# Moving the products of head rows with their inverse norms from VectorE to GpSimd in a two-layer decoder trunk

## The chip, the cores and the metric

The kernel runs on one core of a Trainium2 chip. The metric is the time of one execution on the device in microseconds (us). The core has a matrix engine (TensorE, PE in the profile; PEld is its weight load), VectorE (DVE), ScalarE (ACT), GpSimd (POOL), SyncE (SP), and DMA queues. SP issues most loads; POOL issues one kind of DMA, described below.

## The reference

Two layers are run over a sequence of 256 tokens with width 2048. Each layer has two groups of eight heads that share one input projection and one output projection, and an MLP of 8192:

```
h    = rms_norm(x, attn_norm)
proj = h @ w_in            # g_q g_k g_v g_gate g_lr | s_q s_k s_v
log_a = log_sigmoid(g_lr @ w_gate_up + b_gate) / 16
o_gla = gla_chunked(heads(g_q), heads(g_k), heads(g_v), heads(log_a))
o_gla = rms_norm(o_gla, gla_out_norm) * silu(g_gate)        # norm per head
sq, sk = rms_norm(heads(s_q), sb_q_norm), rms_norm(heads(s_k), sb_k_norm)
o_sb  = rms_norm(stick_breaking_attention(sq, sk, heads(s_v)), sb_out_norm)
x = x + concat(o_gla, o_sb) @ w_o
x = x + square(relu(rms_norm(x, mlp_norm) @ w_up)) @ w_down
```

A head has 128 columns. Four tensors in each layer are therefore normalised head by head: the stick-breaking queries, their keys, their outputs, and the outputs of the gated linear attention (GLA).

## The kernel before

Everything is float32. A large product is made of three matmuls of parts: each operand is split into a high part and the low rest, and high times high, high times low and low times high are summed (L1243 to L1245 for the narrow products of the input projection, with the weight parts `whi` and `wlo`). SP loads raw weights; ACT makes `whi` (L868); DVE makes `wlo` as raw minus `whi` (L872). In the MLP some low parts, `dlo`, are made another way: ACT writes the negated high part (L876) and a DMA that POOL issues adds the raw weights to it (L879).

All work of a layer is written as pieces of a `Plan`: a piece has an engine, an assumed length, the pieces that it depends on and the buffers that it takes and frees. `Plan.run` gives each piece a due time. PE's pieces that are written in line are due one after the other at their assumed lengths; a piece on another engine is due in time for its earliest user. Then `run` plays the pieces through: DVE and ACT take the ready piece with the earliest due time; PE, SP and POOL take the pieces of their `line` in the order in which they were written. PE pieces that are set `apart` (turns, scores, and so on of the attention) go ahead of PE's line as soon as they are ready in the plan. The order that comes out is fixed on every engine; at run time semaphores alone hold an engine back. Inside the attention stage, `core` adds pieces of the attention, `into_bank` adds a PE piece that writes into a PSUM bank, `aside` one that is set apart.

`heads_norm(rows, w)` norms rows of 128 tokens by `w` columns, that is `w`/128 heads: ACT squares each row (L1348), DVE sums each head's squares (L1351), `inv_rms` makes the inverse root of the mean (DVE L459, ACT, then three short DVE steps at L466 to L468 that refine it), and `mul_heads` multiplies the row by its heads' inverse norms (L1330, one DVE tensor_tensor of 128x512 a row). The kernel runs it on pairs of rows of 512 columns for keys and queries (512 columns is four heads, so twice for eight heads), on the stick-breaking outputs `on`, and on the GLA outputs: 16 products in each layer. Whoever uses a row waits for its product: `heads_turn` transposes keys and queries on PE (L1378) for the scores; the outputs `on` and the GLA outputs, those after a multiplication with the gate (DVE), are transposed into the output projection's operand (`to_operand`, PE L1519).

The gates of the GLA need the low-rank columns `lr`: DVE scales them (L2021), PE turns them (L1681), DVE copies the result into `lrT` (L1687), and PE multiplies it by `wg` (L1701). POOL makes masks and cleared tiles at the start of a layer and memsets of the padded GLA operands `act` and `t` (L1792, L1793, L1891), and copies decay factors `dec` (L1747).

Of the kernel before, what the change touches and what calls it, by code (L numbers as in the profile page):

```python
# [33 lines left out]
FASTR = (1, 3, 4, 5, 6)  # L34
ADDEDR = (2, 7)
FIRSTR = 1
STEPSI = [0, 0, 1, 3, 1, 2, 2, 1, 1, 3, 4, 4, 5, 5, 5, 6, 5, 6, 6, 6, 7, 7]
FASTI = (1, 5, 6)
ADDEDI = ADDED
# [22 lines left out]
class Plan:  # L62
# [48 lines left out]
    def release(self, hold, *pieces):  # L111
        for p in Plan.flat(pieces):
            p.frees.append(hold)
            hold.left += 1

    def run(self, stock):
        for p in self.pieces:
            p.deps = Plan.flat([p.deps, p.after])
            for d in p.deps:
                d.users.append(p)  # L120
        t = 0.0
        for p in self.pieces:
            if p.engine == "PE":
                t += p.length
                p.due = t - p.length
        wait = {p: len(p.deps) for p in self.pieces}
        topo = [p for p in self.pieces if not p.deps]
        for p in topo:
            for u in p.users:
                wait[u] -= 1  # L130
                if not wait[u]:
                    topo.append(u)
        assert len(topo) == len(self.pieces)
        for p in reversed(topo):
            if p.engine != "PE" or p.apart:
                p.due = min([u.due for u in p.users], default=t) - p.length - p.lag - self.GAP
        for p in self.pieces:
            if p.core:
                p.due -= EARLY
        line = {  # L140
            e: [p for p in self.pieces if p.engine == e and not p.apart]
            for e in ("PE", "SP", "POOL")
        }
        free = dict.fromkeys(("PE", "SP", "POOL", "DVE", "ACT", "NONE"), 0.0)
        left = {p: len(p.deps) for p in self.pieces}
        at = dict.fromkeys(self.pieces, 0.0)
        ready = {"DVE": [], "ACT": [], "NONE": [], "APART": []}
        pool = {k: list(v) for k, v in stock.items()}
        order, events, count = [], [], 0
        for p in self.pieces:  # L150
            if not p.deps:
                events.append((0.0, count, p))
                count += 1
        came = set()

        def fits(p):
            return all(
                sum(h.kind == k for h in p.takes) <= len(v) for k, v in pool.items()
            ) if p.takes else True

        def first_fit(heap):
            put_back, got = [], None
            while heap:
                c = heapq.heappop(heap)
                if fits(c[2]):
                    got = c[2]
                    break
                put_back.append(c)
            for c in put_back:
                heapq.heappush(heap, c)  # L170
            return got

        while events:
            now, _, p = heapq.heappop(events)
            if isinstance(p, Plan.Piece):
                e = "APART" if p.apart else p.engine
                if e in ready:
                    heapq.heappush(ready[e], (p.due, count, p))
                else:
                    came.add(p)  # L180
                count += 1
            elif p is not None:
                for h in p:
                    pool[h.kind].append(h.m)
            for e in free:
                if free[e] > now + 1e-9:
                    continue
                p = first_fit(ready[e]) if e in ready else None
                if e == "PE":
                    p = first_fit(ready["APART"])  # L190
                if not p and e in line and line[e] and line[e][0] in came and fits(line[e][0]):
                    p = line[e].pop(0)
                if not p:
                    continue
                for h in p.takes:
                    h.m = pool[h.kind].pop(0)
                order.append(p)
                free[e] = now + p.length
                heapq.heappush(events, (free[e], count, None))
                count += 1  # L200
                got = p.gives
                for h in p.frees:
                    h.left -= 1
                    if not h.left:
                        got = got + [h]
                if got:
                    heapq.heappush(events, (free[e] + p.lag + self.GAP, count, got))
                    count += 1
                for u in p.users:
                    gap = self.SAME.get(e, 0.0) if u.engine == e else self.GAP  # L210
                    if u.apart and u.engine != e:
                        gap += self.CALM
                    at[u] = max(at[u], free[e] + p.lag + gap)
                    left[u] -= 1
                    if not left[u]:
                        heapq.heappush(events, (at[u], count, u))
                        count += 1
        assert len(order) == len(self.pieces)
        for p in order:
            if p.fn:  # L220
                p.fn()
        return max(free.values())
# [3 lines left out]
def trunk_kernel(  # L226
# [17 lines left out]
    nc = tc.nc  # L244
# [57 lines left out]
    def t2_tile(hold=None, shape=(P, 512)):  # L302
        if hold is None:
            m = turn_of[0] = (turn_of[0] + 1) % T2
        else:
            m = hold.m
        return tpool.tile(list(shape), F32, tag=f"t2_{m}", name=nm("t"), bufs=1)
# [426 lines left out]
    def lazy(make):  # L734

        box = []

        def get():
            if not box:
                box.append(make())  # L740
            return box[0]

        return get
# [39 lines left out]
    def unit_order(u):  # L783

        if u.kind == "o":
            return (STEPSO, STEPSP)[u.n2], (FASTO0, FASTO)[u.n2]
        if u.kind in ROWS[FIRSTR:]:
            return STEPSR, FASTR
        if u.kind == ROWS[0]:
            return STEPSI, FASTI  # L790
        return STEPS, FAST
# [477 lines left out]
    def core(engine, length, fn, *deps, lag=0.0):  # L1269
        p = add(engine, length, fn, *deps, opened["att"], lag=lag)  # L1270
        p.core = True
        using["att"].append(p)
        return p
# [38 lines left out]
    def norm_tile(key, hold, n):  # L1312
        tile_ = spool.tile([P, 8], F32, tag=f"{key}{hold.m}", name=nm("st"), bufs=1)
        return tile_[:, :n]
# [11 lines left out]
        b = core("ACT", 0.42, lambda: box["parts"][1](), a)  # L1326
        return (lambda: box["rr"]), core("DVE", 0.72, lambda: box["parts"][2](), b)

    def mul_heads(dst, src, rr, nh):
        nc.vector.tensor_tensor(  # L1330
            dst.rearrange("p (h d) -> p h d", d=P),
            src.rearrange("p (h d) -> p h d", d=P),
            rr.unsqueeze(2).to_broadcast([P, nh, P]),
            ALU.mult,
        )

    def heads_norm(rows, w, *deps):

        nh = w // P
        slot_hold = Plan.Hold("norm")  # L1340
        ss = lazy(lambda: norm_tile("ns", slot_hold, len(rows) * nh))
        got = []
        for i, (row, dep) in enumerate(rows):
            hold = Plan.Hold("t2")
            sq = lazy(lambda hold=hold: t2_tile(hold))

            def square(row=row, sq=sq):
                nc.scalar.activation(sq()[:, :w], row(), AF.Square)  # L1348

            def total(i=i, sq=sq):  # L1350
                nc.vector.tensor_reduce(  # L1351
                    ss()[:, i * nh : (i + 1) * nh],
                    sq()[:, :w].rearrange("p (h d) -> p h d", d=P), AX.X, ALU.add,
                )

            a = core("ACT", 0.2 + w * 8.3e-4, square, dep, *deps)
            a.takes.append(hold)
            got.append(core("DVE", 0.14 + w * 1.06e-3, total, a, got))
            release(hold, got[-1])
        got[0].takes.append(slot_hold)  # L1360
        rr, ready = inv_rms(ss, len(rows) * nh, P, slot_hold, got)
        muls = [
            core(
                "DVE", 0.15 + w * 1.06e-3,
                lambda i=i, row=row: mul_heads(row(), row(), rr()[:, i * nh : (i + 1) * nh], nh),
                ready,
            )
            for i, (row, _) in enumerate(rows)
        ]
        release(slot_hold, muls)  # L1370
        return muls
# [796 lines left out]
```

## Time and profile before

| | |
|---|---|
| median of three runs | 2127.96 us (2127.22 to 2128.28) |
| the profiled execution | 2126.1 us |
| its span | 2124.3 us |
| PE busy | 2113.5 us, 99% |
| DVE busy | 1970.3 us, 93% |
| ACT busy | 1599.6 us, 75% |
| POOL busy | 175.6 us, 8% |
| granted TensorE clock | 1.0 |

The span is the time between the first and the last instruction of the profile; what the execution takes beyond it is the launch around it. A share is the busy time over the span. The two attention stages, where all products of inverse norms lie, are at about 198 to 305 us and 1234 to 1330 us. A row of a group has line, engine, operation, output<-inputs with partitions x elements, the count, then busy us and mean ns of one. A row of a timeline has start, length, engine and line; what stands in brackets at its end is the idle time before it and what ended that.

### The profile page before, as it was taken

What the parts mean: (1) busy time and instruction counts of PE and PEld (TensorE: products, weight loads), DVE (VectorE), ACT (ScalarE), POOL (GpSimd) and SP (SyncE); (2) the same over time, 40 slices, a digit from 0 to 9 for tenths busy, and PEclk for the clock granted to TensorE, in tenths of its full rate; (3) what the DMA queues carried; (4) which work ended last, traced back from release to release, by engine and by line L of the source; (5) the groups of instructions that cost most, each with busy time, mean ns of one, the idle gap of its engine ahead of it and who ended that gap; (6) DMA issues with size and microseconds to landing.
All of it is one profiled execution on the core that took longest, in us unless ns stands there. A gap on an engine that the chain in (4) does not pass through costs nothing.

```text
span 2124.3 us, 28632 instructions
## 1 busy us (share of the span) xinstructions
PE 2113.5 (99%) x10043; PEld 1759.2 (83%) x10043; DVE 1970.3 (93%) x2672; ACT 1599.6 (75%) x2082; POOL 175.6 (8%) x234
## 2 busy tenths in 40 slices
PE   9999999999999999999999999999999999999999
PEld 8888888888888888888888888888888888888887
DVE  7998889999999999999999987899999999999998
ACT  7776878787678677678787776878876776786775
POOL 0111000000000000000010101000000000000000
PEclk9999999999999999999999999999999999999999
DMA  8897347888888888878888762778888888888786
GB/s 302 246 269 197 128 150 229 253 255 254 268 235 257 241 251 253 268 240 248 234 249 261 222 204 80 224 232 250 262 241 256 254 241 272 236 256 249 250 246 177
DMA packets 160723, 501.35 MB, mean 236 GB/s; under 512 B 14298, under 2 KB 23074, under 8 KB 160580
## 3 DMA queue, kind: packets, MB, share of 16 engines
q1 hardware_dynamic: 135236, 407.25, 55.2%
q0 software_dynamic: 25344, 92.29, 23.0%
q8 instruction: 79, 1.29, 0.2%
q14 instruction: 64, 0.52, 0.1%
HBM read 405.12 MB, written 2.10 MB: 192 GB/s over the span
## 4 chain that ended last, share of the span: by engine, by line
PE 96%; DMA 2%; ACT 1%; DVE 1%; issue 0%; POOLq 0%; DVEq 0%
DMA dlo<-raw 2%; ACT whi L868 0%; PE m__462_2282 L1243 0%; PE m__468_2294 L1243 0%; PE m__2547_12117 L1243 0%; PE m__2549_12123 L1243 0%; DVE wlo L872 0%; DVE act L749 0%; PE m__12_144 L668 0%; PE m__12_144 L667 0%; PE m__579_2863 L1243 0%; PE m__13_145 L667 0%; PE m__579_2863 L1244 0%; PE m__462_2282 L1245 0%; PE m__2473_11750 L1245 0%
## 5 line engine op out<-in xcount | busy, mean ns | idle before, releaser
L868 ACT ACTIVATE whi<-raw 128x1024 fp32r<-128x1024 f32 (+2 forms) x944 | 900.6, 969 | 331.7 <-issue 57.7
L872 DVE TENSOR_TENSOR wlo<-raw,whi 128x1024 fp32r<-128x1024 f32 (+1 forms) x768 | 830.5, 1086 | 69.8 <-ACT whi L868 61.1
L879 POOL DMA_DIRECT2D dlo<-raw x176 | 150.2, 855 | 1760.7 <-ACT dlo L876 974.9
L868 ACT ACTIVATE whi<-ts 128x1024 fp32r<-128x1024 f32 x176 | 186.4, 1059 | 82.4 <-DVE ts L749 5.9
L872 DVE TENSOR_TENSOR wlo<-ts,whi 128x1024 fp32r<-128x1024 f32 x176 | 214.6, 1219 | 6.4 <-ACT whi L868 5.0
L749 DVE TENSOR_TENSOR ts<-raw 128x1024 f32<-128x1024 f32 x176 | 214.6, 1220 | 1.9
L876 ACT ACTIVATE dlo<-raw 128x1024 fp32r<-128x1024 f32 x176 | 180.8, 1046 | 7.8 <-PE m__2004_9526 L968 1.7
L749 DVE TENSOR_TENSOR raw<-raw 128x512 f32<-128x512 f32 x176 | 120.7, 686 | 1.7
L749 DVE TENSOR_TENSOR raw<-ts,raw 128x512 f32<-128x512 f32 x176 | 120.3, 683 | 0.2
L1106 ACT ACTIVATE act<-act,st 128x512 f32<-128x512 f32 x96 | 66.4, 713 | 30.9 <-DVE act L749 30.6
L541 DVE TENSOR_TENSOR act<-t,act 128x512 fp32r<-128x512 f32 (+1 forms) x97 | 60.9, 635 | 0.1
L537 ACT ACTIVATE act<-t 128x512 fp32r<-128x512 f32 (+1 forms) x97 | 55.7, 583 | 0.4
L1351 DVE TENSOR_REDUCE st<-t 128x4 f32<-128x512 f32 x32 | 21.1, 680 | 7.1 <-ACT t L1348 7.1
L749 DVE TENSOR_TENSOR xb<-t,xb 128x512 f32<-128x512 f32 x40 | 27.3, 683 | 0.2
L610 ACT ACTIVATE t<-xb 128x512 f32<-128x512 f32 x32 | 20.5, 653 | 8.1 <-DVE xb L749 7.7
L541 DVE TENSOR_TENSOR sx<-t,sx 128x384 fp32r<-128x384 f32 (+1 forms) x44 | 23.5, 538 | 0.0
L537 ACT ACTIVATE sx<-t 128x384 fp32r<-128x384 f32 (+1 forms) x44 | 21.8, 500 | 1.3 <-DVE t L519 1.2
L519 DVE TENSOR_TENSOR t<-t,t 128x128 f32<-128x128 f32 x53 | 15.5, 292 | 1.8
L517 DVE TENSOR_TENSOR t<-t 128x128 f32<-128x128 f32 x53 | 15.4, 290 | 1.5
L1330 DVE TENSOR_TENSOR act<-act,st 128x512 f32<-128x512 f32 x24 | 15.5, 681 | 0.0
L516 DVE TENSOR_TENSOR t<-t 128x128 f32<-128x128 f32 x53 | 15.0, 283 | 0.0
L1348 ACT ACTIVATE t<-act 128x512 f32<-128x512 f32 x24 | 14.4, 620 | 0.1
(4359 smaller groups left out, 6122.8 us busy)
## 6 DMA issues: line engine op xcount, KB each, us to landing
raw<-in_w_up_dram SPq DMA_DIRECT2D x112, 1024.0 KB, 5.1
raw<-in_w_down_dram SPq DMA_DIRECT2D x112, 1024.0 KB, 6.4
dlo<-raw POOLq DMA_DIRECT2D x176, 512.0 KB, 6.2
raw<-in_w_in_dram SPq DMA_DIRECT2D x80, 1024.0 KB, 6.0
raw<-in_w_o_dram SPq DMA_DIRECT2D x30, 1024.0 KB, 8.1
raw<-in_w_up_dram SPq DMA_DIRECT2D x32, 512.0 KB, 6.3
raw<-in_w_down_dram SPq DMA_DIRECT2D x32, 512.0 KB, 5.8
raw<-in_w_in_dram SPq DMA_DIRECT2D x30, 512.0 KB, 5.5
```

The lines of the kernel that those rows point to most:

```text
L519: nc.vector.tensor_tensor(e[0][:, 1, :], a12, e[0][:, 0, :], ALU.subtract)
L537: nc.scalar.activation(d[:, :, 0, :], src, AF.Copy)
L541: nc.vector.tensor_tensor(d[:, :, 1, :], src, f32(d[:, :, 0, :]), ALU.subtract)
L610: nc.scalar.activation(junk, xb[n][:, tt, :], AF.Square, accum_out=ssq[:, tt, n : n + 1])
L749: nc.vector.tensor_tensor(dst, a, b, op)
L868: nc.scalar.activation(view(box["h"]), src(), AF.Copy)
L872: nc.vector.tensor_tensor(view(box["l"]), src(), f32(view(box["h"])), ALU.subtract)
L876: nc.scalar.activation(box["l"], src(), AF.Copy, scale=-1.0)
L879: nc.gpsimd.dma_start(f32(box["l"]), src(), accum_op=ALU.add)
L1106: nc.scalar.activation(box[h][:, tt, :], box[h][:, tt, :], AF.Relu if into else AF.Copy, scale=norm["rr"][:, tt : tt + 1],)
L1330: nc.vector.tensor_tensor(dst.rearrange("p (h d) -> p h d", d=P), src.rearrange("p (h d) -> p h d", d=P), rr.unsqueeze(2).to_broadcast([P, ...
L1351: nc.vector.tensor_reduce(ss()[:, i * nh : (i + 1) * nh], sq()[:, :w].rearrange("p (h d) -> p h d", d=P), AX.X, ALU.add,)
```

## The change

`mul_heads` issues the 32 products on GpSimd in place of VectorE. The plan counts 1.17 us for each (0.15 + 512 x 0.002) where it counted 0.69 (0.15 + 512 x 0.00106). POOL's pieces are no longer taken in the order in which they were written: like DVE's and ACT's they are taken by due time when they are ready.

```diff
@@ the constants @@
+MUL = "POOL"
+MULT = 2e-3
@@ Plan.run @@
         line = {
             e: [p for p in self.pieces if p.engine == e and not p.apart]
-            for e in ("PE", "SP", "POOL")
+            for e in ("PE", "SP")
         }
-        ready = {"DVE": [], "ACT": [], "NONE": [], "APART": []}
+        ready = {"DVE": [], "ACT": [], "POOL": [], "NONE": [], "APART": []}
@@ the norms of heads @@
-    def mul_heads(dst, src, rr, nh):
-        nc.vector.tensor_tensor(
+    def mul_heads(engine, dst, src, rr, nh):
+        engine.tensor_tensor(
@@ heads_norm @@
             core(
-                "DVE", 0.15 + w * 1.06e-3,
-                lambda i=i, row=row: mul_heads(row(), row(), rr()[:, i * nh : (i + 1) * nh], nh),
+                MUL, 0.15 + w * (1.06e-3 if MUL == "DVE" else MULT),
+                lambda i=i, row=row: mul_heads(
+                    nc.gpsimd if MUL == "POOL" else nc.vector,
+                    row(), row(), rr()[:, i * nh : (i + 1) * nh], nh,
+                ),
                 ready,
             )
```

The order that the plan makes differs from the order before only inside the two attention stages. In the new code a line number is higher by 2, and by 5 behind `heads_norm`: L1330 becomes L1332, L1378 L1383, L1243 to L1245 become L1245 to L1247 in the loop of matmuls, L872 becomes L874.

PE in the first layer's projection, before: the transposes of keys (`act_1092`) and queries (`act_1780`) of the first four heads, behind the last narrow matmuls of that part (`m__371`, `m__372`), and then the turn of `lr` and its use.

```order
L1243 MATMUL m__372_1838<-whi_2001,act_304 128x272
L1244 MATMUL m__372_1838<-wlo_2018,act_304 128x272
L1245 MATMUL m__372_1838<-whi_2001,act_304 128x272
L1378 MATMUL m__415_2050<-ident,act_1092 128x128 x4
L1378 MATMUL m__416_2055<-ident,act_1780 128x128 x4
L1378 MATMUL m__418_2062<-ident,act_1092 128x128 x4
L1378 MATMUL m__420_2069<-ident,act_1780 128x128 x4
L1681 MATMUL m__421_2074<-ident,lr_2047 16x128 x2
L1701 MATMUL m__425_2084<-lrT_1887,wg_1853 128x256 x2
```

What stands there at the same number of narrow matmuls now, from 21 narrow matmuls before the old place of the transposes on.

```order
L1246 MATMUL m__371_1833<-wlo_2009,act_293 128x272
L1247 MATMUL m__371_1833<-whi_1991,act_293 128x272
L1383 MATMUL m__412_2020<-ident,act_1092 128x128 x4
L1383 MATMUL m__413_2025<-ident,act_1092 128x128 x4
L1245 MATMUL m__372_1838<-whi_1991,act_293 128x272
L1246 MATMUL m__372_1838<-wlo_2009,act_293 128x272
L1247 MATMUL m__372_1838<-whi_1991,act_293 128x272
```

The keys' transposes moved ahead of 21 narrow matmuls. The queries' follow 12 narrow matmuls behind the keys' second, and the low-rank turn of `lr` went further back.

DVE in the same place, before, from the last refining step of the queries' inverse norms on (the keys' are in `st_1948`):

```order
L468 SCALAR_TENSOR_TENSOR st_1951<-st_1952,st_1951 128x8
L1330 TENSOR_TENSOR act_1092<-act_1092,st_1948 128x512
L872 TENSOR_TENSOR wlo_2006<-raw_1830,whi_1990 128x2x272
L1330 TENSOR_TENSOR act_1092<-act_1092,st_1948 128x512
L872 TENSOR_TENSOR wlo_2018<-raw_1830,whi_2001 128x2x272
L1330 TENSOR_TENSOR act_1780<-act_1780,st_1951 128x512 x2
L1597 COPY gcol_b<-m__405_1966 128x40
L1599 SCALAR_TENSOR_TENSOR gqk<-gcol_b 128x2
```

and now:

```order
L470 SCALAR_TENSOR_TENSOR st_1951<-st_1952,st_1951 128x8
L1602 COPY gcol_b<-m__405_1966 128x40
L1604 SCALAR_TENSOR_TENSOR gqk<-gcol_b 128x2
L874 TENSOR_TENSOR wlo_2009<-raw_1830,whi_1991 128x2x272
L874 TENSOR_TENSOR wlo_2018<-raw_1830,whi_2004 128x2x272
L2026 TENSOR_SCALAR lr_2070<-m__371_1833,st_752 128x16
L2026 TENSOR_SCALAR lr_2070<-m__372_1838,st_752 128x16
```

The four products are gone from DVE, the two short pieces `gcol` and `gqk` moved ahead, and `wlo_2009`, with which PE's row of that name works, follows straight behind them.

POOL in the first layer, before:

```order
L325 MEMSET kdz_1885 128x1536
L372 MEMSET lrT_1887 17x256
L1747 COPY dec_2143<-eg_2140 128x8
L1891 MEMSET t_2585 64x4x64 x2
L1792 MEMSET act_2478 64x2x256
L1793 MEMSET act_2478 64x2x256
L1747 COPY dec_2143<-eg_2140 128x8
L1792 MEMSET act_2516 64x2x256
```

and now, with the products of keys and queries of both halves:

```order
L327 MEMSET kdz_1885 128x1536
L374 MEMSET lrT_1887 17x256
L1332 TENSOR_TENSOR act_1092<-act_1092,st_1948 128x512 x2
L1332 TENSOR_TENSOR act_1780<-act_1780,st_1951 128x512 x2
L1332 TENSOR_TENSOR act_1093<-act_1093,st_2258 128x512 x2
L1332 TENSOR_TENSOR act_1781<-act_1781,st_2263 128x512 x2
L1752 COPY dec_2305<-eg_2302 128x8
L1896 MEMSET t_2647 64x4x64 x2
L1752 COPY dec_2305<-eg_2302 128x8
```

The eight products of keys and queries stand ahead of the first `dec` copy. `dec` copies and the memsets of `t` and `act` come in another order than before. The DMAs for `dlo` stand in the order of before.

PE in the second layer, at the same transposes, before:

```order
L1243 MATMUL m__2388_11323<-whi_11425,act_10010 128x272
L1244 MATMUL m__2388_11323<-wlo_11441,act_10010 128x272
L1245 MATMUL m__2388_11323<-whi_11425,act_10010 128x272
L1378 MATMUL m__2424_11489<-ident,act_10579 128x128 x4
L1378 MATMUL m__2426_11496<-ident,act_10579 128x128 x4
L1243 MATMUL m__2387_11319<-whi_11484,act_10104 128x272
L1244 MATMUL m__2387_11319<-wlo_11494,act_10104 128x272
L1245 MATMUL m__2387_11319<-whi_11484,act_10104 128x272
```

and now:

```order
L1247 MATMUL m__2388_11323<-whi_11425,act_10010 128x272
L1245 MATMUL m__2387_11319<-whi_11484,act_10104 128x272
L1246 MATMUL m__2387_11319<-wlo_11486,act_10104 128x272
L1247 MATMUL m__2387_11319<-whi_11484,act_10104 128x272
L1383 MATMUL m__2426_11496<-ident,act_10579 128x128 x4
L1383 MATMUL m__2428_11504<-ident,act_10579 128x128 x4
L1245 MATMUL m__2388_11323<-whi_11484,act_10104 128x272
```

There the keys' transposes moved three narrow matmuls back, and the low weight part of the first of them is now the first thing that PE needs there.

PE at the use of the low-rank turn, first layer, now (`hA` holds attention weights, `m__459` an output of the stick-breaking heads):

```order
L1686 MATMUL m__458_2269<-ident,lr_2070 16x128 x2
L1496 MATMUL m__459_2272<-act_732,hA_2248 128x128
L1500 MATMUL m__459_2272<-act_732,hA_2248 128x128
L1504 MATMUL m__459_2272<-act_732,hA_2248 128x128
L1496 MATMUL m__459_2272<-act_732,hA_2248 128x128
L1500 MATMUL m__459_2272<-act_732,hA_2248 128x128
L1504 MATMUL m__459_2272<-act_732,hA_2248 128x128
L1706 MATMUL m__461_2288<-lrT_1887,wg_1853 128x256 x2
```

Six matmuls of the stick-breaking outputs stand between the turn of `lr` (L1686) and its use (L1706), where before the two stood one behind the other.

## The prediction

> **What bounds the kernel now.** I read the first part of the page for the busy shares, then PE's list of waits, then the groups by form for the price of a product, and last the timelines of the places where products stand.
>
> From the page:
>
> ```profile
> span 2124.3 us, 28632 instructions
> PE 2113.5 (99%) x10043; PEld 1759.2 (83%) x10043; DVE 1970.3 (93%) x2672; ACT 1599.6 (75%) x2082; POOL 175.6 (8%) x234
> ```
>
> PE is busy in 2113.5 of 2124.3 us, so 10.8 us of idle time is all that better feeding could win. DVE is the next busiest, GpSimd (POOL) nearly empty. What PE's idle time waited for stands in the view of waits of PE (total us, count, longest):
>
> ```profile
> PE m__4_97 L621 <- POOL ident masks.py:199: 1.4, 1, 1.4
> PE m__4027_19088 L968 <- DMA dlo<-raw: 1.1, 1, 1.1
> PE m__1367_6557 L968 <- DMA dlo<-raw: 1.1, 1, 1.1
> PE m__425_2084 L1701 <- DVE lrT L1687: 0.6, 1, 0.6
> PE m__2387_11319 L1244 <- DVE wlo L872: 0.5, 1, 0.5
> PE m__371_1833 L1244 <- DVE wlo L872: 0.5, 1, 0.5
> ```
>
> PE waits for DVE three times that show: 0.6 + 0.5 + 0.5 = 1.6 us. The two for `wlo` stand at the projection's part that the first head norms run beside, ahead of their first product; only the low-rank wait (L1701) comes after products. The largest two that are left wait for `dlo` transfers, and the first for the identity at the start. No product delays PE in this trace.
>
> **What the change takes off DVE.** From the groups by form, with the two stages' windows behind them (us; then busy time and count of PE, PEld, DVE, ACT, POOL; clock; DMA share):
>
> ```profile
> L1330 DVE TENSOR_TENSOR act<-act,st 128x512 f32<-128x512 f32 x24 | 15.5, 681 | 0.0
> L1330 DVE TENSOR_TENSOR on<-on,st 128x512 f32<-128x512 f32 x8 | 5.3, 686 | 0.0
> 198.00:305.00 107.00, 105.21 (x722) 90.62 (x720) 85.80 (x170) 82.69 (x149) 5.99 (x15) 1.00 0.42 140
> 1234.00:1330.00 96.00, 95.39 (x681) 83.91 (x680) 75.54 (x144) 71.31 (x129) 5.71 (x14) 1.00 0.42 136
> ```
>
> All 32 products, 15.5 + 5.3 = 20.8 us, leave DVE, 10.4 in each attention stage. DVE is busy there 85.80 of 107.00 and 75.54 of 96.00 us, so it has 21.2 and 20.5 us to spare already and PE gains nothing from the sum: it is hidden under PE's 105.21 and 95.39. On GpSimd it adds 16 products a layer to some 6 us of work; the queue stays mostly empty. Behind a product on that queue stand the copies of `dec` and the memsets of the linear attention, and, after the last product of a stage, `dlo` issues in the same order as before: at nothing, since 16 x 1.17 + 6 = 24.7 of 107 us leaves 82 us of cover; were the products to come late in a bunch, a `dlo` would pay as in the two waits of 1.1.
>
> **How long a product takes on GpSimd.** No product runs there in this trace. The nearest rows, the first three from the groups by form and the rest from the timelines of GpSimd and DVE (start, us):
>
> ```profile
> masks.py:199 POOL TENSOR_SCALAR_AFFINE_SELECT ident<-ident 128x128 f32<-128x128 f32 x1 | 0.3, 288 | 0.1
> L348 POOL TENSOR_SCALAR_AFFINE_SELECT t<-t 128x128 f32<-128x128 f32 x2 | 4.0, 2020 | 0.1
> L1793 POOL MEMSET act<- 64x512 f32 x4 | 2.1, 521 | 0.1
> ...
> 1097.97 2.72 POOL L348 TENSOR_SCALAR_AFFINE_SELECT t<-t 128x128 f32<-128x128 f32 x1
> 1097.50 0.68 DVE L749 TENSOR_TENSOR raw<-ts,raw 128x512 f32<-128x512 f32 x1
> 1098.10 0.68 DVE L872 TENSOR_TENSOR wlo<-raw,whi 128x512 fp32r<-128x512 f32 x1
> 1098.70 0.68 DVE L749 TENSOR_TENSOR raw<-raw 128x512 f32<-128x512 f32 x1
> 1099.31 1.22 DVE L872 TENSOR_TENSOR wlo<-ts,whi 128x1024 fp32r<-128x1024 f32 x1
> 1100.44 0.26 DVE L466 TENSOR_TENSOR st<-st 128x2 f32<-128x2 f32 x1
> ```
>
> A memset of 512 elements a partition (written only) takes 0.52: the lower end. A select that reads and writes 128 elements takes 0.288 with DVE idle; four times that is 1.15. With twice as much for the second operand it would be 2.3, the upper end. I take 1.17, near the select, the only row that also reads. In a sentence apart: the Trainium skill's "GPSIMD Engine Reference", § 3.1, gives 4497 ns for a tensor_tensor of 2048 columns, against 2293 on VectorE; a quarter is an estimate of 1.12, and the sum by it is the same to 0.1 us a product.
>
> The second price is the neighbour. The same select took 2.72 us from 1097.97: it ended at 1100.69, just where DVE's run of adjoining tensor_tensors, each with operands in SBUF, first paused (1100.44 + 0.26 = 1100.70). Alone it took 0.288. So a GpSimd instruction that reads SBUF stands still while DVE goes from one such instruction to the next. Whether DVE also stands still behind GpSimd no row shows; the bounds are 0 and the product's whole 1.17, and I let both happen in turn below. The Trainium skill's "SBUF — State Buffer", § Who interferes with whom, says that a DVE instruction with two SBUF inputs and a GpSimd instruction that reads SBUF exclude each other for the whole instruction, whichever starts first. The select's row agrees for GpSimd's side; by the page the sum would be the walks below, and without it rival C.
>
> **Layer 0, the first norms.** Timelines of DVE, then PE:
>
> ```profile
> 203.49 0.17 DVE L468 SCALAR_TENSOR_TENSOR st<-st,st 128x8 f32<-128x8 f32 x1
> 203.58 0.72 DVE L872 TENSOR_TENSOR wlo<-raw,whi 128x544 fp32r<-128x544 f32 x1
> 204.61 0.17 DVE L468 SCALAR_TENSOR_TENSOR st<-st,st 128x8 f32<-128x8 f32 x1
> 204.69 0.68 DVE L1330 TENSOR_TENSOR act<-act,st 128x512 f32<-128x512 f32 x1
> 207.17 1.28 DVE L1330 TENSOR_TENSOR act<-act,st 128x512 f32<-128x512 f32 x2
> ...
> 207.04 0.29 PE L1244 MATMUL m__371_1833<-wlo,act 128*128 128x272 f32 x1
> 207.16 0.29 PE L1245 MATMUL m__371_1833<-whi,act 128*128 128x272 f32 x1
> 209.92 0.60 PE L1378 MATMUL m__415_2050<-ident,act 128*128 128x128 f32 x4
> 210.35 0.60 PE L1378 MATMUL m__416_2055<-ident,act 128*128 128x128 f32 x4
> 212.62 1.13 PE L1701 MATMUL m__425_2084<-lrT,wg 17*128 17x256 f32 x4 [0.57 <-DVE lrT L1687]
> ```
>
> The keys' inverse norms are there at 203.49 + 0.17 = 203.66, the queries' at 204.78. Before, the turns of keys and queries (L1378) stood together from 209.92, 1.5 us behind the last product (207.17 + 1.28 = 208.45). In the new order the keys' turns stand 21 narrow matmuls earlier, 0.125 us each (207.04 to 207.16): 209.92 - 2.63 = 207.30. The queries' follow 12 narrow matmuls and two turns (0.44 each) later, at 209.67. So the plan has given away 2.6 us of slack while each product grows by 0.49. Two walks:
> - GpSimd takes each gap of DVE: keys 204.40 to 205.57 and 205.75 to 206.92, the first query product 207.15 to 208.32, and the `wlo` that PE needs at 207.04 only then, by 209.0: PE stands 2.0.
> - DVE keeps its run: first key product 204.80 to 205.97, `wlo` to 206.7, second key product to 207.87 (0.57 late), the next `wlo` to 208.6, the query products to 210.9, wanted at 209.67 + 0.57 = 210.24 (0.66 late): 1.2.
>
> I take the middle, **+1.6**.
>
> **Layer 1, the same place.** DVE, ACT, PE:
>
> ```profile
> 1239.19 0.17 DVE L468 SCALAR_TENSOR_TENSOR st<-st,st 128x8 f32<-128x8 f32 x1
> 1239.89 1.89 DVE L1330 TENSOR_TENSOR act<-act,st 128x512 f32<-128x512 f32 x3
> 1241.70 0.72 DVE L872 TENSOR_TENSOR wlo<-raw,whi 128x544 fp32r<-128x544 f32 x1
> ...
> 1239.28 1.19 ACT L868 ACTIVATE whi<-raw 128x544 fp32r<-128x544 f32 x2
> 1241.69 0.60 PE L1378 MATMUL m__2424_11489<-ident,act 128*128 128x128 f32 x4
> 1244.07 0.60 PE L1378 MATMUL m__2430_11521<-ident,act 128*128 128x128 f32 x4
> ```
>
> Inverse norms come at 1239.36, and PE wants the keys at 1241.69 plus the three narrow matmuls that are now ahead of them, 1242.07, and the queries at 1244.45: 2.7 us for two products of 1.17, and in the same 2.7 us DVE must make two `wlo` from the `whi` that ACT finishes at 1239.93 and 1240.47 (two in 1.19 from 1239.28). If DVE goes first it is done by 1241.3, the key products end at 1242.5 and 1243.65, 1.6 late, and the queries fit behind. If GpSimd goes first, a `wlo` wanted at 1241.81 comes 1.4 to 2.3 late. **+1.6**.
>
> **The rest.** The low-rank wait of 0.57 goes, as six output products now stand between its turn (L1681) and its use (L1701): **-0.6**. Four later places a layer (the second half of keys and queries, the stick-breaking outputs `on`, the gated rows) lose the same 0.49 or more a product, but the plan knows the length; each may cost 0 (the product comes in time) to 1.2 (it is late by one `wlo` of 1.22 us, as in the select's row). I take 0.4 a layer, nearer the lower end, as PE's list of waits shows none of them today: **+0.8**. That GpSimd's pieces go by due time rather than in program order moves no `dlo` issue past another, so nothing.
>
> Sum: 1.6 + 1.6 - 0.6 + 0.8 = **+3.4 us**. The profiled execution took 2126.1 (1.8 around its span), 1.9 under the median of 2127.96; the new profile would read 2129.5 and the median 2131.4.
>
> **Rivals.** 0.2%, or 4.26 us, is about what a measurement of this kernel can tell from no change.
> - B, slower: the later places are late after all. They are on PE's path with no reserve in a new order packed to GpSimd's planned 1.174, and one lock costs one `wlo`, 1.22. Two to six of them give 1.6 + 1.6 - 0.6 = 2.6 plus 2.4 to 7.3, so +5.0 to +9.9, time 2133 to 2138. For it: the select's 2.72 against 0.288, ten times; against: DVE is idle for a fifth of the stage. It decides once the later places cost 1.7 together. Middle 2135.
> - C, no contention (GpSimd reads while DVE reads) and a product near 0.52 to 1.17: the products come in time, the low-rank wait goes and at most one of the `wlo` waits shrinks: -1.1, time 2126.9. Against it: the select's row.
> - E, faster by over 0.2%: takes 4.26 of 10.8 us of idle time, so also the `dlo` waits, which needs their issues to land earlier. Nothing moves them: those issues stand in the same order, outside these stages.
>
> **Chances.** The forecast (+1.3 to +4.2) 0.42; B 0.41; C, with nothing at all, 0.13; E 0.04. Faster 0.04, the same 0.55, slower 0.41. The forecast's own range is 2129.3 to 2132.2. The range given runs from C's 2127.0 to 2138.5, which leaves out E, the lower part of C and the worst of B.
>
> **What would show it.** Right: products of 1.1 to 1.3 us on GpSimd when DVE pauses and 2 or more beside `wlo`; new waits of PE at the keys' turns for the products or at L1244 for `wlo`, 1 to 2 us in each layer; DVE busy about 21 us less; PE busy the same. Wrong: no wait of PE for a product (then C), products near 2.3 us alone, or several waits at outputs and gated rows (then B).

## The result, and the profile after

The changed kernel takes 2133.53 us (median of 8 runs, 2132.28 to 2134.40) against 2127.40 us (8 runs, 2125.72 to 2128.68) for the kernel before: 6.1 us slower, ratio 1.003 with a 95% interval of 1.0021 to 1.0039. Its profiled execution took 2134.15 us.

The first lines of the page of the changed kernel:

```profile
span 2132.4 us, 28664 instructions
PE 2116.3 (99%) x10043; PEld 1761.5 (83%) x10043; DVE 1968.4 (92%) x2640; ACT 1599.4 (75%) x2082; POOL 217.1 (10%) x266
```

Two things stand in the second line. DVE has 32 instructions less and is busy only 1.9 us less (1970.3 before), though the products took 20.8 us there. And PE is busy 2.8 us more with the same matmuls. PE's waits after (total us, count, longest):

```profile
PE m__628_3118 L970 <- DMA dlo<-raw: 4.3, 1, 4.3
PE m__371_1833 L1246 <- DVE wlo L874: 1.5, 2, 1.1
PE m__4_97 L623 <- POOL ident masks.py:199: 1.4, 1, 1.4
PE m__4027_19088 L970 <- DMA dlo<-raw: 1.2, 1, 1.2
PE m__1055_5101 L970 <- DMA dlo<-raw: 1.0, 1, 1.0
PE m__2387_11319 L1246 <- DVE wlo L874: 0.8, 2, 0.5
```

No wait names a product. The first row is new and is the largest in the trace: the first `dlo` of the first layer's output projection. The second row has one new wait of 1.1 us, the sixth one of 0.3. The low-rank wait (L1701 before) is gone.

**The 4.3 us.** Timeline of PE around it:

```profile
313.55 0.39 PE L969 MATMUL m__628_3118<-whi,act 128*128 128x512 f32 x1
318.21 0.80 PE L970 MATMUL m__628_3118<-dlo,act 128*128 128x512 f32 x1 [4.26 <-DMA dlo<-raw]
318.80 0.63 PE L971 MATMUL m__628_3118<-whi,act 128*128 128x512 f32 x1
319.23 0.63 PE L969 MATMUL m__630_3129<-whi,act 128*128 128x512 f32 x1
...
323.92 0.46 PE L971 MATMUL m__628_3118<-whi,act 128*128 128x512 f32 x1
324.22 0.40 PE L969 MATMUL m__628_3118<-whi,act 128*128 128x512 f32 x1
324.45 0.39 PE L970 MATMUL m__628_3118<-wlo,act 128*128 128x512 f32 x1
```

Behind the wait the matmuls start 0.43 us apart (318.80 to 319.23) until 323.92, where they otherwise start 0.23 apart (324.22 to 324.45): some 2.8 us on top, and PE's extra busy time. The windows of that stretch show it as a granted clock of 0.93 and 0.90:

```profile
300.00:320.00 20.00, 15.73 (x68) 12.69 (x67) 15.58 (x25) 16.35 (x24) 1.75 (x2) 0.93 0.88 292
320.00:340.00 20.00, 20.00 (x85) 16.32 (x84) 15.59 (x29) 13.30 (x19) 1.72 (x2) 0.90 0.49 136
```

What changed ahead of that `dlo` is the order of the raw loads. Timelines of SP's queue, the first four loads for the output projection, after:

```profile
271.34 0.37 SPq L842 DMA_DIRECT2D raw<-in_w_o_dram  x1
297.09 0.37 SPq L842 DMA_DIRECT2D raw<-in_w_o_dram  x1
297.55 0.42 SPq L842 DMA_DIRECT2D raw<-in_w_o_dram  x1
298.06 0.42 SPq L842 DMA_DIRECT2D raw<-in_w_o_dram  x1
```

and the same loads before the change, the second and third in one row:

```profile
287.02 0.37 SPq L840 DMA_DIRECT2D raw<-in_w_o_dram  x1
287.48 0.94 SPq L840 DMA_DIRECT2D raw<-in_w_o_dram  x2
```

The third load after (297.55) fills the tile of which the first two `dlo` are both made; before the change it stood second (287.48), and the load behind it, the fourth after, stood third. The load that now stands ahead of these two goes into a tile that an older `wlo` must free. The waits of SP's queue from 290 to 297.3 us, and that `wlo` in DVE's timeline:

```profile
SPq L842 <- DVE wlo L874: 25.3, 1, 25.3
295.81 1.22 DVE L874 TENSOR_TENSOR wlo<-raw,whi 128x1024 fp32r<-128x1024 f32 x1
```

So SP stood 25.3 us at the head of its queue, the two loads behind it left 10 us later than before, and three loads left within 1 us. GpSimd's issue of the first `dlo`, before and after, and the time in us from the issue to the landing after (last number):

```profile
304.06 0.87 POOL L879 DMA_DIRECT2D dlo<-raw  x1 [37.36 <-ACT dlo L876]
309.31 0.88 POOL L881 DMA_DIRECT2D dlo<-raw  x1 [11.38 <-ACT dlo L878]
dlo<-raw POOLq DMA_DIRECT2D x1, 512.0 KB, 8.9
```

The later issue is not the work of the late load. Its raw weights landed at 306.10 (297.55 + 8.55 in the chain that ended last), and ACT, for which GpSimd waits here, began its part at 307.97 straight behind other pieces of its new order. What the late loads did shows in the length of the transfer, 8.9 us: the run with the loads in written order, below, has nearly the same issue and 4.5.

**GpSimd's products, and what they did to DVE.** Groups by form, after:

```profile
L1332 POOL TENSOR_TENSOR act<-act,st 128x512 f32<-128x512 f32 x24 | 30.8, 1297 | 99.6 <-ACT st L465 31.2 <-DVE st L468 28.8 <-DVE st L470 20.5
L1332 POOL TENSOR_TENSOR on<-on,st 128x512 f32<-128x512 f32 x8 | 9.0, 1126 | 20.4 <-DVE st L468 10.3 <-ACT t L1350 6.2 <-DVE st L470 3.6
```

Timelines of GpSimd, DVE and PE at the first norms of the first layer:

```profile
204.12 2.38 POOL L1332 TENSOR_TENSOR act<-act,st 128x512 f32<-128x512 f32 x2 [14.89 <-ACT st L465]
206.81 2.59 POOL L1332 TENSOR_TENSOR act<-act,st 128x512 f32<-128x512 f32 x2 [0.31 <-DVE st L470]
203.41 0.16 DVE L468 TENSOR_TENSOR st<-st 128x8 f32<-128x8 f32 x1
204.53 1.00 DVE L468 TENSOR_TENSOR st<-st 128x8 f32<-128x8 f32 x1
205.57 0.97 DVE L469 SCALAR_TENSOR_TENSOR st<-st,st 128x8 f32<-128x8 f32 x1
206.88 0.99 DVE L1604 SCALAR_TENSOR_TENSOR gqk<-gcol_b 128x2 f32<-128x2 f32 x1
207.79 2.19 DVE L874 TENSOR_TENSOR wlo<-raw,whi 128x544 fp32r<-128x544 f32 x2
208.56 0.39 PE L1246 MATMUL m__371_1833<-wlo,act 128*128 128x272 f32 x1 [1.06 <-DVE wlo L874]
```

The same step on 128x8 takes 0.16 us at 203.41 and 1.00 us at 204.53, beside a product. Each of the short steps is held for the rest of one product, and the `wlo` that PE needs at 207.5 starts at 207.79. This is DVE's side of the exclusion that the prediction had shown for GpSimd alone. The Trainium skill's "SBUF — State Buffer", § Who interferes with whom, says so for both sides, and here the trace agrees: 0.16 against 1.00 us. So it is not semaphores alone that hold an engine back in this kernel.

### The profile page after: what moved, and what is told of

It reads as the page before. It is cut to its first block, busy times and chain, and to the rows that moved or that the text cites. A ratio compares the mean times of both kernels' runs of the same rounds, so it can differ in the third digit from the quotient of the medians.

```text
span 2132.4 us, 28664 instructions
## 1 busy us (share of the span) xinstructions
PE 2116.3 (99%) x10043; PEld 1761.5 (83%) x10043; DVE 1968.4 (92%) x2640; ACT 1599.4 (75%) x2082; POOL 217.1 (10%) x266
## 4 chain that ended last, share of the span: by engine, by line
PE 95%; DMA 3%; DVE 1%; issue 1%; ACT 0%; POOL 0%; POOLq 0%; DVEq 0%
DMA dlo<-raw 2%; DMA raw<-in_w_o_dram 0%; DVE wlo L874 0%; DVE st L1353 0%; PE m__2546_12107 L1245 0%; PE m__12_144 L670 0%; PE m__462_2298 L1245 0%; DVE act L751 0%; PE m__468_2312 L1245 0%; PE m__12_144 L669 0%; PE m__13_145 L669 0%; PE m__2474_11752 L1245 0%; DVE st L469 0%; PE m__462_2298 L1247 0%; PE m__2472_11746 L1245 0%
## 5 line engine op out<-in xcount | busy, mean ns | idle before, releaser
L874 DVE TENSOR_TENSOR wlo<-raw,whi 128x1024 fp32r<-128x1024 f32 (+1 forms) x768 | 833.9, 1091 | 78.9 <-ACT whi L870 68.8
L874 DVE TENSOR_TENSOR wlo<-ts,whi 128x1024 fp32r<-128x1024 f32 x176 | 214.9, 1221 | 6.8 <-ACT whi L870 6.1
L1332 POOL TENSOR_TENSOR act<-act,st 128x512 f32<-128x512 f32 x24 | 30.8, 1297 | 99.6 <-ACT st L465 31.2
```

Of the source, the lines that this page charges most:

```text
L874: nc.vector.tensor_tensor(view(box["l"]), src(), f32(view(box["h"])), ALU.subtract)
L1332: engine.tensor_tensor(dst.rearrange("p (h d) -> p h d", d=P), src.rearrange("p (h d) -> p h d", d=P), rr.unsqueeze(2).to_broadcast([P, nh ...
```

## The experiments

Each theory's letter is that of the first expectations: L, a late load; C, contention and longer products; O, the new order itself. Every ratio is to the kernel before, run beside it.

**The new order with products on VectorE.** The plan is that of the changed kernel, the products run on DVE at those places. SP's order differs at the place of theory L: the two loads stand ahead of the raw load again.

```diff
-                    nc.gpsimd if MUL == "POOL" else nc.vector,
+                    nc.vector,
```

> The order of PE and ACT is that of the changed kernel, row for row; the 32 products run on VectorE at the places at which the plan put them on GpSimd. SP's order differs at one place: the two raw2 loads for the first layer's output projection stand ahead of the second raw load, as before the change. Theory L (the loss is a late load: in the changed kernel SP stands 25.3 us at a raw load that waits for a wlo, with the two raw2 loads behind it, so that dlo comes 4.3 us late and the clock is low for some 6 us more): no wait for dlo at about 313 us, no low clock, median 2126.5 to 2128.5. Theory C (the loss is contention of GpSimd and VectorE and longer products): also 2126 to 2128, since GpSimd does no products; the wait for wlo of 1.1 us at 208 us goes. Rival O (the new order of PE is the loss): 2131 to 2134.

Measured: 2129.32 us against 2126.90, ratio 1.0008 (0.9999 to 1.0017). Lines of its page, and of its waits of PE:

```profile
PE 2113.2 (99%) x10043; PEld 1757.9 (83%) x10043; DVE 1970.9 (93%) x2672; ACT 1599.4 (75%) x2082; POOL 176.1 (8%) x234
PE m__653_3240 L1524 <- DVE act L1989: 1.8, 1, 1.8
PE m__628_3118 L970 <- DMA dlo<-raw: 0.3, 1, 0.3
```

The 4.3 us are down to 0.3, and both engines' contention is gone. Yet it lies above what L and C give, and below O: the order alone has a wait of 1.8 us, of the transposes of gated rows for the gate's multiplication. In the changed kernel that wait does not show, since the 4.3 us stand ahead of it. Compared with the changed kernel, where PE and ACT have the same order, DVE was busy 1970.9 - 1968.4 = 2.5 us longer. So of 20.8 us moved off DVE 18.3 came back as held instructions, by these two profiled executions.

**The old order with products on GpSimd.** The plan is that of before in all its costs and queues; at the products only the engine is exchanged. Against the kernel before, cut to the lines that matter:

```diff
+MUL = "DVE"
...
-                "DVE", 0.15 + w * 1.06e-3,
-                lambda i=i, row=row: mul_heads(row(), row(), rr()[:, i * nh : (i + 1) * nh], nh),
+                MUL, 0.15 + w * (1.06e-3 if MUL == "DVE" else MULT),
+                lambda i=i, row=row: mul_heads(
+                    nc.gpsimd,
```

> The order of PE, ACT and SP is that of the kernel before, row for row; only the 32 products run on GpSimd. Theory L: no late load, so 2127 to 2129.5 (0 to +2, from products that are longer than the plan counts). Theory C: the loss stays or grows, since the plan counts 0.69 us for products that take 1.0 to 1.9: 2131 to 2135, with new waits of PE at the transposes of keys, queries and outputs.

Measured: 2127.02 against 2126.90, ratio 1.0001 (0.9992 to 1.001). The row of its page, and the one wait of PE for a product:

```profile
PE 2113.7 (99%) x10043; PEld 1759.2 (83%) x10043; DVE 1964.9 (92%) x2640; ACT 1599.8 (75%) x2082; POOL 218.1 (10%) x266
PE m__2430_11521 L1383 <- POOL act L1332: 0.3, 1, 0.3
```

Products that are longer than the plan counts, and a DVE that is held, cost 0.3 us of wait here. Theory C falls as the main cause: in the old order the move of engine neither won nor lost more than the interval's 0.1% (2 us).

**GpSimd's due times alone.** Products stay on DVE:

```diff
-MUL = "POOL"
+MUL = "DVE"
```

> Products stay on VectorE at their old cost; only GpSimd's pieces go by due time. Some memsets and six or so matmuls of the attention change places. All theories: 2126.5 to 2128.5, as before. If it is over 2130, the ordering of GpSimd's pieces is part of the loss.

Measured: 2126.25 against 2126.90, ratio 0.9994 (0.9985 to 1.0003). No part of the loss.

**The loads in written order.** The changed kernel, with each load of the output projection issued behind the one written ahead of it:

```diff
+    queued = {}
...
+            elif u.kind == "o":
+                dep = queued.get("load") if u.l == queued.get("layer") else None
+                with tc.issue_after(dep) if dep else nullcontext():
+                    queued["load"] = nc.sync.dma_start(dst, src).ins
+                queued["layer"] = u.l
             else:
                 nc.sync.dma_start(dst, src)
```

The order of PE, ACT, DVE and GpSimd stays row for row, SP's changes at three places: the one of theory L and two neighbouring pairs in the second layer.

> The changed kernel, but the loads of the output projection's weights are issued in the order in which they are written, so that the two raw2 loads of the first layer stand ahead of the second raw load. Theory L: they go at about 287 to 293.5 us instead of 297.6, dlo is there in time, the 4.3 us wait and the low clock behind it (2.6 us) go: 2126 to 2127.5, 6 to 7 below the changed kernel. Theory C: 2132 to 2134, no change. Rival P: the raw2 loads wait for memory that GpSimd's last products hold until 294 to 298 us, so a part of the wait stays: 2128 to 2133.

Measured: 2131.10 against 2126.90, ratio 1.0016 (1.0007 to 1.0024). The first four loads in SP's timelines, and two of its waits of PE (a line here has a number up to six higher than in the changed kernel):

```profile
271.01 0.37 SPq L845 DMA_DIRECT2D raw<-in_w_o_dram  x1
282.42 0.37 SPq L845 DMA_DIRECT2D raw<-in_w_o_dram  x1
287.30 0.37 SPq L845 DMA_DIRECT2D raw<-in_w_o_dram  x1
296.75 0.37 SPq L845 DMA_DIRECT2D raw<-in_w_o_dram  x1
...
PE m__653_3240 L1530 <- DVE act L1995: 1.9, 1, 1.9
PE m__371_1833 L1252 <- DVE wlo L880: 1.5, 2, 1.1
```

The two loads go 10 to 15 us earlier and the wait of 4.3 us is gone, as L said. But the issue is hardly earlier. The first `dlo` here, with its time to landing, and the DMA from 305 to 309 us (the last two numbers are the engines' busy share and GB/s), in the changed kernel and here:

```profile
308.98 0.88 POOL L887 DMA_DIRECT2D dlo<-raw  x1 [11.39 <-ACT dlo L884]
dlo<-raw POOLq DMA_DIRECT2D x1, 512.0 KB, 4.5
...
305.00:309.00 4.00, 4.00 (x19) 3.30 (x18) 3.10 (x7) 1.98 (x4) 0.00 (x0) 1.00 1.03 414
305.00:309.00 4.00, 4.00 (x19) 3.27 (x19) 2.75 (x7) 2.32 (x4) 0.03 (x1) 1.00 0.81 267
```

The issue is only 0.33 us earlier than in the changed kernel (309.31), the landing 4.7 us: 8.9 - 4.5 = 4.4 us are the transfer's own. With the loads bunched behind 297 us, the DMA engines are still full of raw weights when `dlo` is issued; that they delay it is read from these rates. The later issue itself, 309 instead of 304, belongs to the new order and is harmless here.

Rival P falls: these loads did not have to wait for GpSimd's last products. But only 2.4 us came back by the medians (3 by the ratios, 0.3% to 0.16%), not 6 to 7: the wait of the gated rows, 1.9 us, comes out from behind it, with a low clock of its own. Against the new order on DVE this kernel is 1.8 us slower (2131.10 to 2129.32, same chip; PE and ACT in the same order, SP but for the two pairs of the second layer): that is GpSimd's share in the new order, the 1.1 us at 208 us among it. The eleven executions of each kernel spread over some 5 us, so this share is known only to a us or two, and the clock is in it: 9 of 11 executions have less than 1.00 here, 6 of 11 there.

**Which products, and at which price.** Four plans more, of which one line each is shown. The first two choose the products by the number of rows in a norm, keys and queries (more than one row) and then outputs (one row), and `eng` takes the place of `MUL` at the product; the others change the price, to 3e-3 and to 4e-3:

```diff
+        eng = MUL if len(rows) > 1 else "DVE"
...
+        eng = MUL if len(rows) == 1 else "DVE"
...
-MULT = 2e-3
+MULT = 3e-3
```

> Only the products of keys and queries (8 a layer) go to GpSimd, those of outputs stay on VectorE. In SP's order the two raw2 loads stand ahead of the second raw load. Theory L (late load behind the raw load): no wait for dlo near 313 us, 2126.5 to 2130, what is left being waits that the new order makes. Theory C (contention): half the products, half the loss: 2129.5 to 2131.5, at the transposes of keys and queries.

> Only the products of the outputs (8 a layer) go to GpSimd. In SP's order the two raw2 loads stand ahead of the second raw load. Theory L: no wait for dlo near 313 us, 2126.5 to 2130. Theory C: half the loss or more, since these products stand at the end of the stage: 2129.5 to 2132.

> All 32 products on GpSimd as in the change, but the plan counts 1.69 us for each (0.15 + 512 x 0.003) instead of 1.17. SP's order has the two raw2 loads first. Theory L and order: no wait for dlo near 313 us, 2126.5 to 2130. Theory that the plan's price was too low for the real 1.26 us: 2126 to 2128, and no wait for wlo at 208 us. Theory C: as the changed kernel, 2131 to 2134.

> The plan counts 2.20 us for each product (0.15 + 512 x 0.004). Here SP's order again has the second raw load ahead of the two raw2 loads. Theory L: the raw2 loads stand behind a wait for a wlo and dlo is late again by 2 to 6 us near 313 us, 2130 to 2135, unless that wlo comes by 291 us. Price theory: 2126 to 2128, better than with 1.69. Theory C: 2131 to 2134.

Measured:

| | us | ratio to before (2126.89) | PE's wait for `wlo` at 207 us | for `dlo` near 314 us |
|---|---|---|---|---|
| keys and queries only | 2135.13 | 1.0039 (1.0026 to 1.0051) | 1.0 | 0.2 |
| outputs only | 2124.94 | 0.9990 (0.9981 to 1.0000) | none | none |
| price 3e-3 | 2130.35 | 1.0014 (1.0006 to 1.0023) | 1.0 | none |
| price 4e-3 | 2133.36 | 1.0032 (1.0020 to 1.0045) | 1.0 | 1.0 |

Theory C's "half the products, half the loss" falls: one half loses no less than the whole (1.0039 and 1.003, with intervals that overlap), the other nothing. The price theory falls too, a price above the real 1.25 us (the mean of the 32 products) brings neither 2126 to 2128 nor an end of the wait at 207 us. Theory L holds in sign: of the four only the price of 4e-3 has the raw load ahead of the other two, and only it has a wait for `dlo` of more than 0.2 us there. Its size was missed, 1.0 instead of 2 to 6. Again the transfer is long: `dlo`, issued at 307.4, takes 9.3 us to land. From its waits of PE:

```profile
PE m__623_3101 L970 <- DMA dlo<-raw: 1.0, 1, 1.0
```

The two loads (297.46 and 297.97 in SP's timeline) are as late as in the changed kernel (297.55 and 298.06), but the matmul ahead of that `dlo` starts at 315.3 instead of 313.5 us, and `dlo` is issued 1.9 us earlier.

The wait for `wlo` at 207 us stands in all runs with keys and queries on GpSimd in a plan that was made for it, and not in the new order on DVE nor in the old order on GpSimd. As far as these runs go it takes both: DVE held, and a plan that left no room. The profiled execution of the kernel with keys and queries only is the fastest of its five (2132.94 us, with 1.8 us at the gated rows and 1.8 us for a `dlo` at 1375 us). What the other four, up to 2137.66, lose beyond it no trace shows; their mean granted clock is 0.998 or 0.999, that of the profiled one 0.999.

**The outputs' plan with products on DVE, and once more on GpSimd.** The first is the plan of the run with outputs only, with `nc.vector` for all products.

> The order of PE, ACT and SP of the run with only the outputs' products on GpSimd (which read 2124.94 us, 0.999 of before, 0.9981 to 1.0), but all products on VectorE. If that gain is real and comes from the order: again 2124.5 to 2126. If it comes from VectorE's relief: 2126.5 to 2128. If it was chance: both this and the repeated run 2126 to 2128.

> The run with only the outputs' products on GpSimd once more. Real: 2124.5 to 2126 and a ratio below 0.9998. Chance: 2126 to 2128.

Measured, against 2127.14: on DVE 2124.82, ratio 0.9986 (0.9977 to 0.9995); on GpSimd 2124.98, ratio 0.9989 (0.9980 to 0.9998). The gain of 2.2 us is real and belongs to the order: it is there with no product on GpSimd. PE is busy 2111.5 us in the one on DVE and 2111.7 in the one on GpSimd, DVE 1970.9 and 1966.0. Both are faster than the kernel before by about what a measurement can tell, and clearly faster than the changed kernel.

## Why the prediction was right or wrong

The time lies in the stated range, above the likeliest case's own (2129.3 to 2132.2) and in that of B (2133 to 2138), but not by B's mechanism. That the wide range holds it is luck in part: two waits that the sum had, one that it put at nothing and a slow clock that it did not have make up the loss. The outcome, slower by over 0.2%, had been given 0.41, less than "the same" with 0.55.

- **PE is the bound, DVE's relief wins nothing: right.** The old order on GpSimd measures it at 1.0001. "DVE busy about 21 us less" was wrong: 2.5 us by the pair with the new order, 5.4 by that with the old (1970.3 to 1964.9), 1.9 from the kernel before to the changed one. "PE busy the same" was wrong by the slow clock, 2.8 us. The prediction had DVE's side of the exclusion in its walks and left it out of this sum.
- **A product at 1.17 us, bounds 0.52 to 2.3: right.** The groups have 1.30 and 1.13; the shortest take 1.04. The select of `ident` was not "the only row that also reads", as the select of `t` beside it does so at 2.02 us.
- **Layer 0, +1.6: right in place and in mechanism, smaller in size.** The wait is for `wlo`, as in the walk where GpSimd takes the gaps, 1.06 instead of 2.0. **Layer 1, +1.6:** 0.3; GpSimd held DVE there too, but the `wlo` was only that late.
- **The low-rank wait, -0.6: right.** It is gone.
- **The later places, +0.8, and rival B's two to six late products: wrong.** PE waits for no product. What is late in the new order is the gate's multiplication, 1.8 us. It stands at the gated rows, a place that B names, but with the products on DVE as well, so the order makes it late and not a product on GpSimd.
- **The step that failed is `dlo`, costed at nothing.** The prediction looked at GpSimd's issues, found their order unchanged and stopped, and rival E says that nothing moves them. An order of issues says neither when they come nor how long the transfers take. The issue came 5 us later in the new order, with the products on DVE too (308.25), and the transfer took 8.9 us instead of 4.5, because SP's loads had changed their order: one that had to wait stood ahead of two others, and they left in a bunch. This order was to be had without a run, as the one on PE was. It cost 4.26 us of wait and 2.8 of clock in the trace, 2.4 us net when it was put right.

The sum, by medians beside their own runs of before: the order alone +2.4 (whose interval just takes in zero), GpSimd in that order +1.8, the exchanged loads +1.9, together 6.1. By the ratios the three are 1.7, 1.7 and 3.0, together 6.4, which shows how well each is known. The parts are not independent, since the late `dlo` hides the late gated rows.

Not tried: the order of loads of the changed kernel with all products on DVE, which would say how much of the 25.3 us is due to a held DVE. And why the price of a product changes the places of gated rows by 2 us was not followed through the plan.

## What to carry to other kernels

Where a planner sets the order, a changed price changes it in places far from the change: read the new order of every queue, the loads' too, and ask of a transfer not only when it is issued but what else the DMA engines have in hand until it lands. To tell the engine from the order, run the new order on the old engine and the old order on the new; here that took two kernels and showed the move to be worth nothing in the old order, while the plans that another price or choice of products made lay from -2 to +8 us. And work is off an engine only if the engine that takes it over does not hold it: count what the neighbour's instructions gain in length.

## What the runs showed of the hardware

A tensor_tensor on 128x8 on DVE that takes 0.16 us alone takes 1.00 beside a GpSimd product, so such products are a bad neighbour for a chain of short steps on DVE.

A `dlo` transfer of 512 KB landed 4.5 us after its issue where the DMA moved 267 GB/s just ahead of it, and 8.9 us after it where it moved 414.

The clock fell after shorter waits than expected. With a wait of 1.85 us in the run with the loads in written order, PE's timeline reads:

```profile
320.03 0.39 PE L977 MATMUL m__634_3143<-whi,sx 128*128 128x512 f32 x1
322.26 1.24 PE L1530 MATMUL m__653_3240<-ident,act 128*128 128x128 f32 x4 [1.85 <-DVE act L1995]
...
323.73 0.63 PE L976 MATMUL m__634_3143<-wlo,act 128*128 128x512 f32 x1
324.15 0.63 PE L977 MATMUL m__634_3143<-whi,act 128*128 128x512 f32 x1
```

The starts are 0.42 apart again. In the new order on DVE a wait of 1.80 us at the same place left the clock at 1.00 in the profiled execution, while six of its eleven executions have 0.999; those with 1.00 have a median of 2127.8, those with 0.999 of 2129.7. That this wait lowered the clock there no trace shows: of the 33 executions of the kernel before, beside them, five have 0.999 too. Nor does the length of a wait decide. With the price of 4e-3 a wait of 0.57 us, as long as the low-rank wait of the kernel before, which kept 1.00, has a clock of 0.76 behind it:

```profile
1249.11 1.13 PE L1706 MATMUL m__2436_11548<-lrT,wg 17*128 17x256 f32 x4 [0.57 <-DVE lrT L1692]
1252.00:1256.00 4.00, 4.00 (x28) 3.88 (x26) 2.54 (x3) 3.28 (x6) 0.00 (x0) 0.76 0.88 283
```

The Trainium skill's "TensorE: Matmul & The Clock Gate", § Why this matters for your kernels, asks for no idle gaps over about 3 us; the runs show a low clock after waits of 1.85 and of 0.57 us. What else decides stays open.
